# One decoder layer on one core: the key selection counted by sign sums on ScalarE alone, the mixers' queues laid out with other durations, and the next weights fetched through the mixers' feed

## The chip, the cores and the metric

The kernel runs on one core of a Trainium2 chip. Its engines work side by side, each through a queue of its own in a fixed order: TensorE (PE in the profile, its weight loads PEld), VectorE (DVE), ScalarE (ACT), GpSimd (POOL) and SyncE (SP, which only issues DMAs). The metric is the device time of one execution in microseconds (us): the median of three runs was 2349.24 us (2349.01 to 2350.36). Durations inside the kernel come from one profiled execution.

## The reference

One layer, 1024 tokens, width 1024, all in float32:

```
x = x + 1/2 * SwiGLU_1(RMSNorm(x))
h = RMSNorm(x);  [c_q|k_a|v_a|k_idx|w_idx|q_b|k_b|v_b|g_a|g_b] = h @ W_in
y_a: score[t,s] = sum over 8 heads of w_idx[t,h] * relu(q_idx[t,h] . k_idx[s])   (s <= t)
     the 256 keys of highest score of each token; softmax attention over those alone
y_b: a[t,s] = sigmoid(z[t,s]) * product over s < j < t of (1 - sigmoid(z[t,j])),  o = a @ v_b   (8 heads)
x = x + W_out( sigmoid(g_a) * (y_a @ W_oA) + sigmoid(g_b) * (y_b @ W_oB) )
x = x + 1/2 * SwiGLU_2(RMSNorm(x))
```

The selection is exact: of equal scores the keys that come first are taken until 256 are reached.

## The kernel before

A float32 product is made of three passes of matmuls on a high and a low part of each operand (`mm3`), and the two parts are written by a copy on ACT and a subtraction on DVE or POOL. The layer runs in five stretches: the first feed-forward block (0 to some 650 us), the projections and the **index stage** (to some 980 us), the **sticks stage** (stick-breaking attention, to some 1327 us), the **sparse stage** (attention over the selected keys, output products; to some 1565 us), and the second feed-forward block.

The three middle stages are written by hand: every piece of work is a generator (`Stream`) that names the engine and the tiles that it needs next, and a planner (`Weave`) steps the stream that could start first by its own clock. `Weave.cost` holds the durations that this clock uses; the order in which the streams are stepped is the order of the instructions in each engine's queue. A float in a `yield` is slack: such a piece stands back behind others that could start within that time.

Parts that the change touches:

- `topk` finds each token's 256th highest score. Tokens go in blocks of 128; blocks 0 and 1 have no more than 256 keys and need no search. **Group 0** is blocks 7, 2, 3 (1024, 384 and 512 keys), **group 1** blocks 4, 5, 6 (640, 768 and 896 keys). The threshold T is found bit by bit, 31 bits for each group. In `by_sign` a bit is one pass: for each block an ACT instruction takes the sign of score minus candidate over all keys and adds up the signs (tile `junka`, line 1108, with an accumulator read behind it), then DVE compares the three sums and sets the bit (`m`, `T`, `cand`, lines 1105 to 1112). Group 1 does 31 such passes, group 0 the upper 15. Its lower 16 bits are counted on DVE: the low halves of the scores whose upper half equals T are put in a tile `word`, and each bit is one DVE count for each block (tile `junkv`, line 1142).
- Where fewer than 256 scores are at or above zero, the search runs on negated scores: `flip` multiplies the score tiles (`u`) by `sig` (+1 or -1) before the search and again after it (line 1078).
- After the search, the **closing** of a group compares, counts, scans (`eq`, `gt`, `cum`, lines 1176 to 1189) and writes a tile of 0 and -1e30, `bias`, to DRAM (`bd`). The sparse stage's logits wait for both groups (`top0`, `top1`), and their DVE piece `e` (line 1699) reads the bias.
- `sticks`: for each head and half (c = 1 is token blocks 4 to 7, c = 0 blocks 0 to 3), scores on PE (`psz`), two sigmoids on ACT (`left`, `sa`), a product scan and a multiplication on DVE (`left`, `sa`), transposes on PE (`pstT`), their split on ACT and DVE (`pt`), products with the values (`psy`). `y_out` ends a half: it splits y into `yh` and `yl`, the subtraction being on POOL (line 1615).
- `fillers` are projections (`psf`) that PE does in between; `Feed` fetches and splits their weights, three sets ahead.
- At the end of the sparse stage `project("oa")` makes 8 outputs (`psoa`), each copied by ACT (`o`), multiplied and added on POOL and stored (`md`); behind them come the products `psm`, whose weights `woa` are fetched by `wcols` outside the planner.

Of the kernel before, what the change touches and what calls it, by code (L numbers as in the profile page):

```python
# [10 lines left out]
F32 = mybir.dt.float32  # L11
# [12 lines left out]
P = 128  # L24
# [6 lines left out]
H = 8  # L31
# [26 lines left out]
def f32(ap):  # L58
    return ap.bitcast(F32)
# [34 lines left out]
class Weave:  # L94
# [8 lines left out]
    COST = {PE: (0.015, 2400.0), DVE: (0.12, 960.0), ACT: (0.1, 1250.0), POOL: (0.2, 465.0)}  # L103

    def __init__(self, nc):
# [4 lines left out]
        self.streams, self.own, self.last = [], None, 0.0  # L110

    def cost(self, i, eng, outs, ins):
        fixed, rate = self.COST[eng]
        n = max([a.free_size() for a in outs[:1] + ins], default=1)
        if eng == PE:
            n = max(outs[0].free_size(), 240)
        else:
            fixed += (0.3 if eng == ACT else 0.08) * (len(outs) > 1)
        if eng == POOL and n <= H:
            fixed += 0.15 + 0.145 * n  # L120
        if eng == DVE:
            wide = [a for a in outs[:1] + ins if a.free_size() > 1]
            if getattr(i, "is_tensor_tensor_scan", False):
                n *= 2
            elif not any(a.space == PSUM for a in wide) and len(wide) <= 2:
                n *= (0.5 if any(a.dtype in (F32, F32R, I32) for a in wide) else 0.25) * len(outs)
        return fixed + n / rate
# [6 lines left out]
    def flush(self):  # L134
        traced = self.nc.cur_bb.bb.instructions
        for i in traced[self.seen:]:
# [6 lines left out]
            if any(a.space == DRAM for a in outs + ins):  # L143
                mb = prod(outs[0].shape) * 4e-6
                if eng == SP:
                    self.free[SP] = max(self.free[SP], t) + mb / 0.25
                    t, eng = self.free[SP] + 3.0, "DMA"
# [3 lines left out]
            else:  # L151
                t = max(t, self.free[eng]) + self.cost(i, eng, outs, ins)
# [68 lines left out]
def trunk(ctx, tc, x, positions, g_ffn1, w1_gate, w1_up, w1_down, g_mix, w_in, g_cq, w_uq_a, w_q_idx,  # L221
# [664 lines left out]
    with fp as fpool, fps as fpsum, psm as psum, tc.manual_schedule(  # L886
# [77 lines left out]
        sets += [(w, d * P, 2 * P, 0, 4, f"{nm}{d}") for w, nm in ((w_o_b, "ob"), (w_o_a, "oa")) for d in range(0, ND, 2)]  # L964

# [94 lines left out]
        def topk(group, gi):  # L1060
# [8 lines left out]
            def count(op, th):  # L1069
                for b, i in enumerate(group):  # L1070
                    yield DVE
                    nc.vector.tensor_scalar(junks[0][:, 0:(i + 1) * P], score[i], th if th == 0.0 else th[:, b:b + 1], 0.0,
                                            op0=op, op1=ALU.add, accum_out=cnt[:, b:b + 1])

            def flip():
                for b, i in enumerate(group):
                    yield DVE
                    nc.vector.tensor_scalar(score[i], score[i], sig[:, b:b + 1], None, op0=ALU.mult)

            def halves(b, i):  # L1080

                nk = (i + 1) * P
                return score[i].bitcast(U16)[:, 0:2 * nk:2], score[i].bitcast(BF16)[:, 1:2 * nk:2]

            yield DVE, *[f"score{i}" for i in group]
            yield from count(ALU.is_ge, 0.0)
# [3 lines left out]

            for b, i in enumerate(group):
                nk = (i + 1) * P
                a, d = (2 * TOPK - 1.0 - nk) / 2, (nk + 1.0) / 2
                c = slice(b, b + 1)
                nc.vector.tensor_scalar(kth[:, c], sig[:, c], a, d, op0=ALU.mult, op1=ALU.add)
                nc.vector.tensor_scalar(thr[:, c], kth[:, c], 2.0, -float(nk), op0=ALU.mult, op1=ALU.add)
            yield from flip()


            def by_sign(bits):  # L1100
# [15 lines left out]
            yield from by_sign(range(30, 15, -1))  # L1116
            if gi:
                yield from by_sign(range(15, -1, -1))
            else:
                yield DVE, "stick"  # L1120
                words = []

                above, low, clow = tl("above"), tl("low"), tl("clow")
                for b, i in enumerate(group):
# [941 lines left out]
```

## Time and profile before

| what | us |
|---|---|
| median of the runs (lowest, highest) | 2349.24 (2349.01, 2350.36) |
| the profiled execution's own time | 2345.06 |
| its span, first to last instruction | 2343.0 |
| busy in the span: PE, PEld, DVE, ACT, POOL | 2216.0, 1813.7, 1629.6, 1067.8, 935.9 |
| mean granted TensorE clock | 0.98 of full |

A busy share over the whole span mixes stages with different limits. The two feed-forward blocks are busy on PE nearly throughout and no line of them changes; the table by stage below is the one to read. Busy time of an engine counts overlapping instructions once. The cost of a DMA issue on ACT is not in its busy time.

### The profile page before, as it was taken

What the parts mean: (1) busy time and instruction counts of PE and PEld (TensorE: products, weight loads), DVE (VectorE), ACT (ScalarE), POOL (GpSimd) and SP (SyncE); (2) the same over time, 40 slices, a digit from 0 to 9 for tenths busy, and PEclk for the clock granted to TensorE, in tenths of its full rate; (3) what the DMA queues carried; (4) which work ended last, traced back from release to release, by engine and by line L of the source; (5) the groups of instructions that cost most, each with busy time, mean ns of one, the idle gap of its engine ahead of it and who ended that gap; (6) DMA issues with size and microseconds to landing.
All of it is one profiled execution on the core that took longest, in us unless ns stands there. A gap on an engine that the chain in (4) does not pass through costs nothing.

```text
span 2343.0 us, 30206 instructions
## 1 busy us (share of the span) xinstructions
PE 2216.0 (95%) x10460; PEld 1813.7 (77%) x10460; DVE 1629.6 (70%) x2596; ACT 1067.8 (46%) x2042; POOL 935.9 (40%) x675
## 2 busy tenths in 40 slices
PE   7999999999999988978998699979999999999999
PEld 6788888888888777756777588867878888888877
DVE  5765666688872688799989788833476666667675
ACT  4323233244462468766784565623332323233443
POOL 2554555332253433312332211376345555543233
PEclk9999999999999999998999899989999999999999
DMA  5233333586754323634454522457323333358755
GB/s 163 85 109 95 108 95 108 175 315 227 177 185 140 112 85 104 155 97 88 118 129 120 184 72 80 140 198 257 122 63 99 104 101 102 104 163 287 239 163 178
DMA packets 251497, 330.64 MB, mean 141 GB/s; under 512 B 19536, under 2 KB 154336, under 8 KB 251344
## 3 DMA queue, kind: packets, MB, share of 16 engines
q1 hardware_dynamic: 234224, 288.83, 40.6%
q0 software_dynamic: 7488, 24.16, 2.8%
q10 hardware_dynamic: 9632, 15.73, 1.9%
q8 instruction: 82, 1.34, 0.2%
q14 instruction: 71, 0.58, 0.1%
HBM read 234.78 MB, written 93.88 MB: 140 GB/s over the span
## 4 chain that ended last, share of the span: by engine, by line
PE 69%; DVE 16%; issue 5%; DMA 4%; ACT 4%; POOL 2%; SPq 0%; ACTq 0%; DVEq 0%; POOLq 0%
PE p L649 6%; PE p L650 6%; PE p L648 6%; PE pc L439 3%; PE pc L441 3%; PE pc L440 3%; PE pd L441 3%; PE pd L439 3%; PE pd L440 3%; PE pa L441 3%; PE pa L439 3%; PE pa L440 3%; DVE left L1549 2%; PE pb L439 2%; PE pb L441 2%
## 5 line engine op out<-in xcount | busy, mean ns | idle before, releaser
L1108 ACT ACTIVATE junka<-u,cand 128x640 bf16<-128x640 f32 (+1 forms) x138 | 124.5, 902 | 40.0 <-DVE cand L1105 35.3
L1549 DVE TENSOR_TENSOR_SCAN left<-left 128x640 f32<-128x640 f32 (+3 forms) x64 | 94.4, 1477 | 1.4 <-ACT left L1541 1.2
L1615 POOL TENSOR_TENSOR yl<-yl,yh 64x512 fp32r<-64x512 f32 x16 | 32.3, 2022 | 149.1 <-ACT yh L1611 149.1
L1649 PE MATMUL pstT<-ident,sa 128*128 128x128 f32 x288 | 52.0, 295 | 41.9 <-DVE sa L1552 28.9
L1649 PEld LDWEIGHTS pstT<-ident,sa 128*128 128x128 f32 x288 | 37.2, 150 | 57.1 <-DVE sa L1552 31.2
L1855 POOL TENSOR_TENSOR o<-o,gate 128x512 f32<-128x512 f32 x24 | 30.8, 1285 | 112.1 <-ACT o L1850 109.9
L1552 DVE TENSOR_TENSOR sa<-sa,left 128x639 f32<-128x639 f32 (+3 forms) x64 | 63.5, 994 | 3.4
L1596 ACT ACTIVATE pt<-pstT 128x512 fp32r<-128x512 f32 (+1 forms) x96 | 45.7, 491 | 43.9 <-PE pstT L1649 38.9
L1711 ACT ACTIVATE e<-e,nm 128x768 f32<-128x768 f32 (+7 forms) x64 | 49.4, 774 | 21.2 <-DVE nm L1706 20.6
L1598 DVE TENSOR_TENSOR pt<-pspT,pt 128x512 fp32r<-128x512 f32 x72 | 47.0, 685 | 16.3 <-ACT pt L1596 16.2
L1598 DVE TENSOR_TENSOR pt<-pstT,pt 128x512 fp32r<-128x512 f32 (+1 forms) x96 | 50.6, 548 | 10.5 <-ACT pt L1596 10.1
L1462 DVE SCALAR_TENSOR_TENSOR u<-relu,WI,u 128x512 f32<-128x512 f32 (+1 forms) x70 | 49.1, 716 | 10.2 <-ACT relu L1455 9.3
L649 PE MATMUL p<-bT,bS 128*128 128x512 f32 x132 | 52.7, 399 | 2.7 <-DVE bT L350 2.7
L650 PE MATMUL p<-bT,bS 128*128 128x512 f32 x132 | 52.4, 399 | 0.8 <-POOL bS L350 0.8
L1541 ACT ACTIVATE left<-psz 128x512 f32<-128x512 f32 (+2 forms) x96 | 46.1, 497 | 15.2 <-DVE sa L1552 6.2
L1699 DVE CUSTOM_DVE_ANT_0 e<-psL,bias 128x512 f32<-128x512 f32 (+3 forms) x96 | 50.0, 551 | 3.4 <-PE psL L1738 3.3
L649 PE MATMUL p<-aT,aS 128*128 128x512 f32 x132 | 51.7, 392 | 0.0
L650 PE MATMUL p<-aT,aS 128*128 128x512 f32 x132 | 50.9, 393 | 0.0
L1596 ACT ACTIVATE pt<-pspT 128x512 fp32r<-128x512 f32 x72 | 40.0, 594 | 22.4 <-PE pspT L1792 22.0
L1455 ACT ACTIVATE relu<-psdot 128x512 f32<-128x512 f32 (+1 forms) x80 | 39.6, 521 | 19.1 <-DVE u L1462 13.4
L1543 ACT ACTIVATE sa<-psz 128x512 f32<-128x512 f32 (+2 forms) x96 | 46.5, 502 | 3.5 <-ACT evg L1028 2.4
L648 PE MATMUL p<-bT,bS 128*128 128x512 f32 x132 | 46.4, 392 | 0.0
(3064 smaller groups left out, 8376.6 us busy)
## 6 DMA issues: line engine op xcount, KB each, us to landing
aw<-in_w_down_dram SPq DMA_DIRECT2D x33, 512.0 KB, 4.4
bw<-in_w_down_dram SPq DMA_DIRECT2D x33, 512.0 KB, 4.5
a0r<-in_w_gate_dram SPq DMA_DIRECT2D x22, 512.0 KB, 4.2
a1r<-in_w_up_dram SPq DMA_DIRECT2D x22, 512.0 KB, 4.7
b0r<-in_w_gate_dram SPq DMA_DIRECT2D x22, 512.0 KB, 4.0
b1r<-in_w_up_dram SPq DMA_DIRECT2D x22, 512.0 KB, 4.9
x<-in_x_dram SPq DMA_DIRECT2D x16, 512.0 KB, 6.1
gd<-evg ACTq DMA_DIRECT2D x32, 256.0 KB, 2.3
```

What stands on the lines that cost most here:

```text
L439: nc.tensor.matmul(ps, a[:, c], b[k][:, HI], start=start and k == 0, stop=False, skip_group_check=True)
L440: nc.tensor.matmul(ps, a[:, c], b[k][:, LO], start=False, stop=False, skip_group_check=True)
L441: nc.tensor.matmul(ps, a[:, l], b[k][:, HI], start=False, stop=k == 3, skip_group_check=True)
L648: nc.tensor.matmul(ps[q][m], S[:, h], T[:, HI], start=p == 0, stop=False)
L649: nc.tensor.matmul(ps[q][m], S[:, h], T[:, LO], start=False, stop=False)
L650: nc.tensor.matmul(ps[q][m], S[:, l], T[:, HI], start=False, stop=p == last)
L1108: nc.scalar.activation(junks[1][:, 0:(i + 1) * P], score[i], AF.Sign, bias=cand.bitcast(F32)[:, b:b + 1], accum_out=cnt[:, b:b + 1])
L1549: nc.vector.tensor_tensor_scan(back, back, back, 1.0, op0=ALU.mult, op1=ALU.bypass)
L1552: nc.vector.tensor_mul(a[:, 0:nk - 1], a[:, 0:nk - 1], left[:, 1:nk])
L1596: nc.scalar.activation(pt[:, off:512], tp[:, off:512], AF.Copy)
L1598: nc.vector.tensor_sub(pt[:, 512 + off:1024], tp[:, off:512], f32(pt[:, off:512]))
L1649: nc.tensor.transpose(tp[:, q * P:(q + 1) * P], A[n + q][:, j * P:(j + 1) * P], ident)
```

## The change

Three edits. (1) `topk`: group 0's lower 16 bits are counted by the same sign passes as the others, so that `word`, its counts and the accounts around them go; the scores are no longer turned, and instead each ACT sign instruction takes `scale=sig` beside its bias, and the closing works on the unturned scores with a corrected threshold (6 to 8 more instructions on 128x3 tiles for each group). A sign has slack 2.0. (2) `Weave.cost` gets other durations, a delay behind each result, a slower PE behind a pause, and a mutual slowing of DVE and POOL where both work in SBUF; so the order of all queues in the three middle stages changes, with the same work but for edit 1. In `y_out` the subtraction moves from POOL to DVE. (3) The first two `woa` weight sets are put behind the feed's list and fetched and split by it.

```diff
     def cost(self, i, eng, outs, ins):
-        fixed, rate = self.COST[eng]
+
         n = max([a.free_size() for a in outs[:1] + ins], default=1)
         if eng == PE:
-            n = max(outs[0].free_size(), 240)
...
+            return 0.01 + max(outs[0].free_size(), 240) / 2350, 0.0
+        if eng == ACT:
+            return 0.055 + n / 1190 + 0.22 * (len(outs) > 1), 0.1 + 0.15 * (len(outs) > 1)
...
+                cost, late = self.cost(i, eng, outs, ins)
+                if eng == PE:
+
+                    if t > self.free[PE] + 2.5:
+                        self.cold = 12
+                    self.cold -= 1
+                    cost += 0.85 * cost * (self.cold >= 0)
...
+                t += cost
                 self.free[eng] = self.last = t
+                t += late
...
+        sets += [(w_o_a, d * P, 2 * P, 0, 4, f"woa{d}") for d in (0, 2)]
...
-            yield from flip()
...
-                        yield ACT, cand, score[i]
+                        yield ACT, cand, score[i], 2.0
                         nc.scalar.activation(junks[1][:, 0:(i + 1) * P], score[i], AF.Sign,
-                                             bias=cand.bitcast(F32)[:, b:b + 1], accum_out=cnt[:, b:b + 1])
+                                             scale=sig[:, b:b + 1], bias=cand.bitcast(F32)[:, b:b + 1],
+                                             accum_out=cnt[:, b:b + 1])
...
-            yield from by_sign(range(30, 15, -1))
-            if gi:
-                yield from by_sign(range(15, -1, -1))
-            else:
...
-                for bit in range(15, -1, -1):
-                    nc.vector.tensor_scalar(clow, low, float(1 << bit), None, op0=ALU.add)
-                    for b, i in enumerate(group):
-                        yield DVE, 4.0
-                        nk = (i + 1) * P
-                        nc.vector.tensor_scalar(junks[0][:, 0:nk], words[b].bitcast(U16)[:, 0:nk], clow[:, b:b + 1], 0.0,
-                                                op0=ALU.is_ge, op1=ALU.add, accum_out=cnt[:, b:b + 1])
...
+            yield from by_sign(range(30, -1, -1))
...
-            yield POOL, yl, yh
-            nc.gpsimd.tensor_tensor(yl[0:HD], yt, f32(yh[0:HD]), op=ALU.subtract)
+            yield DVE, yl, yh
+            nc.vector.tensor_tensor(yl[0:HD], yt, f32(yh[0:HD]), op=ALU.subtract)
+            yield POOL, yl
             put_low(ybd[1][h * HD:(h + 1) * HD, cols], yt)
...
+        first = [feed().parts for n in range(2)]
...
-                wh, wl = wcols(w_o_a, d * P, 2 * P, 0, 4, f"woa{d}")
+                wh, wl = first.pop(0) if first else wcols(w_o_a, d * P, 2 * P, 0, 4, f"woa{d}")
```

Where the order moves, three places. The first is ACT's queue early in the sticks stage, between the first and the second head's sigmoids. Names with `cnt_6016` are group 0's signs, with `cnt_6023` group 1's. Before:

```order
L1541 ACTIVATE left<-psz 128x512 x2
L1543 ACTIVATE sa<-psz 128x512 x2
L1108 ACTIVATE junka,cnt_6023<-u_7221,cand_6028 128x640
L1541 ACTIVATE left<-psz 128x128
L1108 ACTIVATE junka,cnt_6023<-u_7538,cand_6028 128x768
L1543 ACTIVATE sa<-psz 128x128
L1108 ACTIVATE junka,cnt_6023<-u_7862,cand_6028 128x896
L1028 ACTIVATE evg<-psf 128x512
```

The same place in the changed program:

```order
L1526 ACTIVATE left<-psz 128x128
L1528 ACTIVATE sa<-psz 128x128
L1118 ACTIVATE junka,cnt_6023<-u_7854,cand_6028,sig_6024 128x896
L1118 ACTIVATE junka,cnt_6016<-u_6820,cand_6021,sig_6017 128x1024
L1118 ACTIVATE junka,cnt_6016<-u_7004,cand_6021,sig_6017 128x384
L1118 ACTIVATE junka,cnt_6016<-u_7131,cand_6021,sig_6017 128x512
L1581 ACTIVATE pt<-pstT 128x512 x2
```

Both groups' signs now stand between the sigmoids and the splits, up to six of them in a row. From the first `left` to the table load for the exponentials there are 75 signs in ACT's queue before, and 128 after.

The second place is DVE's queue where the sticks stage ends and the sparse stage's first `e` begins; `uvraw` is a tile laid over memory of the stage that ends. Before:

```order
L1598 TENSOR_TENSOR pt<-pstT,pt 128x512
L1607 TENSOR_TENSOR yl<-psy,yl 64x512
L1598 TENSOR_TENSOR pt<-pstT,pt 128x384
L1598 TENSOR_TENSOR pt<-pstT,pt 128x256
L1598 TENSOR_TENSOR pt<-pstT,pt 128x128
L1699 ISA e,mx<-psL,bias 128x512
```

The changed program:

```order
L1168 SCALAR_TENSOR_TENSOR eq<-cum,rem_11674,eq 128x768
L1170 TENSOR_TENSOR gt<-gt,eq 128x768
L1174 TENSOR_SCALAR cum<-gt 128x768
L1161 TENSOR_SCALAR eq<-u_7854,T_6027 128x896
L1163 TENSOR_SCALAR gt,cnt_6023<-u_7854,T_6027 128x896
L1164 TENSOR_SCALAR rem_11674<-cnt_6023 128x1
L1166 SCALAR_TENSOR_TENSOR cum<-eq 128x896
L1168 SCALAR_TENSOR_TENSOR eq<-cum,rem_11674,eq 128x896
L1170 TENSOR_TENSOR gt<-gt,eq 128x896
L1174 TENSOR_SCALAR cum<-gt 128x896
L1657 MEMSET uvraw 128x1024
L1685 ISA e,mx<-psL,bias 128x512
```

Group 1's closing, which before was spread among the last three heads, now stands whole behind the last splits and in front of the first `e`.

The third place is PE's queue at the end of the sparse stage, just ahead of the last products `psya` that the remaining `psoa` stand behind (`oa0` and `oa2` are weight sets). Before:

```order
L280 MATMUL psoa<-yah_11599,oa0h 128x512
L281 MATMUL psoa<-yal_11603,oa0h 128x512
L282 MATMUL psoa<-yah_11599,oa0l 128x512
L280 MATMUL psya<-oh_13815,uvh 128x256
L281 MATMUL psya<-ol_13816,uvh 128x256
```

The changed program:

```order
L302 MATMUL psoa<-yah_11448,oa2h 128x512
L303 MATMUL psoa<-yal_11452,oa2h 128x512
L304 MATMUL psoa<-yah_11448,oa2l 128x512
L302 MATMUL psya<-oh_13869,uvh 128x256
L303 MATMUL psya<-ol_13870,uvh 128x256
```

Before, 24 of the 96 `psoa` matmuls (two of the eight outputs) stand ahead of the last `psya`; after, 36 (three).

## Rows read from the trace of the kernel before

**Rows 1.** Windows by stage: us, busy of each engine (instructions), clock, DMA share, GB/s.

```profile
core 0: us, PE busy (x) PEld busy (x) DVE busy (x) ACT busy (x) POOL busy (x), PEclk, DMA share, GB/s
790.00:981.50 191.50, 169.03 (x823) 136.52 (x823) 156.47 (x304) 137.31 (x283) 74.32 (x69) 0.96 0.42 116
981.50:1326.80 345.30, 300.35 (x1467) 238.71 (x1466) 317.74 (x552) 237.13 (x509) 89.52 (x51) 0.94 0.47 122
1326.80:1352.00 25.20, 14.61 (x53) 10.08 (x52) 16.41 (x56) 12.58 (x22) 5.05 (x5) 0.66 0.36 102
1352.00:1515.00 163.00, 162.76 (x913) 139.08 (x913) 140.76 (x431) 105.35 (x229) 38.69 (x38) 1.00 0.27 87
1515.00:1565.00 50.00, 36.23 (x149) 28.19 (x148) 6.25 (x11) 12.49 (x20) 37.39 (x32) 0.86 0.71 244
```

**Rows 2.** Windows of single heads (1024-wide scan to the next), and ACT's fullest stretch.

```profile
998.90:1051.00 52.10, 42.35 (x199) 33.12 (x199) 50.26 (x109) 36.05 (x77) 9.56 (x6) 0.93 0.40 97
...
1271.80:1305.40 33.60, 29.65 (x158) 23.03 (x156) 30.93 (x40) 18.54 (x42) 6.23 (x4) 1.00 0.57 200
...
1185.00:1218.00 33.00, 30.89 (x164) 24.61 (x163) 27.87 (x50) 29.07 (x67) 6.88 (x6) 1.00 0.52 128
```

**Rows 3.** Groups by line on DVE, 780 to 1340 us: count, busy us, mean ns.

```profile
L1598 DVE TENSOR_TENSOR pt<-pstT,pt 128x512 fp32r<-128x512 f32 x48 | 31.8, 681 | 7.5 <-ACT pt L1596 7.3
...
L1142 DVE TENSOR_SCALAR_CACHE_REDUCE junkv<-word,clow 128x1024 bf16<-128x1024 uint16 x16 | 20.4, 1274 | 0.2
...
L1142 DVE TENSOR_SCALAR_CACHE_REDUCE junkv<-word,clow 128x512 bf16<-128x512 uint16 x16 | 11.8, 740 | 0.2
...
L1607 DVE TENSOR_TENSOR yl<-psy,yl 64x512 f32<-64x512 f32 x16 | 10.8, 677 | 2.2 <-ACT yl L1605 2.2
...
L1142 DVE TENSOR_SCALAR_CACHE_REDUCE junkv<-word,clow 128x384 bf16<-128x384 uint16 x16 | 9.7, 605 | 0.1
...
L1112 DVE SCALAR_TENSOR_TENSOR T<-m,T 128x3 int32<-128x3 int32 x46 | 8.6, 186 | 1.6
```

**Rows 4.** Groups by line on ACT: the signs (780 to 1340 us).

```profile
L1108 ACT ACTIVATION_READ_ACCUMULATOR junka<-u,cand 128x1 f32 x138 | 26.9, 195 | 0.0
...
L1108 ACT ACTIVATE junka<-u,cand 128x1024 bf16<-128x1024 f32 x15 | 17.3, 1153 | 10.5 <-DVE cand L1105 10.1 <-ACT evh L1016 0.4
L1108 ACT ACTIVATE junka<-u,cand 128x512 bf16<-128x512 f32 x15 | 10.8, 721 | 0.2
...
L1108 ACT ACTIVATE junka<-u,cand 128x384 bf16<-128x384 f32 x15 | 9.2, 615 | 0.4
```

**Rows 5.** Groups on ACT, whole span: a PSUM copy with a scale column, and without.

```profile
L330 ACT ACTIVATE mhi<-pst,gcolm 128x512 fp32r<-128x512 f32 x16 | 9.8, 694 | 0.0
...
L349 ACT ACTIVATE aT<-pst 128x512 fp32r<-128x512 f32 x16 | 8.3, 598 | 16.1 <-PE pst L399 16.1
```

**Rows 6.** Windows, 1205 to 1290 us: DVE on tile `eq`: us, busy, clock, DMA, GB/s.

```profile
1205.00:1290.00 85.00, 14.88 (x12) 0.98 0.47 127
```

**Rows 7.** Groups on DVE, 1205 to 1291 us.

```profile
L1072 DVE TENSOR_SCALAR_CACHE_REDUCE junkv<-u,cand 128x640 bf16<-128x640 f32 (+2 forms) x3 | 3.0, 1006 | 0.0
...
L1178 DVE TENSOR_SCALAR_CACHE_REDUCE gt<-u,T 128x640 f16<-128x640 f32 (+2 forms) x3 | 3.0, 997 | 0.0
```

**Rows 8.** Timeline of the turn to the sparse stage; in brackets the wait ahead.

```profile
1337.40 0.91 DVE L1671 MEMSET uvraw<- 128x1024 f32 x1 [3.23 <-issue]
...
1339.59 0.63 PE L1792 MATMUL pspT<-ident,e 128*128 128x128 f32 x2
```

**Rows 9.** Instructions on `bd`, DMA from issue to landing.

```profile
DMA to landing us min/median/max: 1.9/2.9/8.2
```

**Rows 10.** The page: groups, whole span.

```profile
L1699 DVE CUSTOM_DVE_ANT_0 e<-psL,bias 128x512 f32<-128x512 f32 (+3 forms) x96 | 50.0, 551 | 3.4 <-PE psL L1738 3.3
```

**Rows 11.** Waits from 1515 to 1565 us: in total, times, longest.

```profile
ACT o L1850 <- DMA md<-o: 12.7, 3, 7.3
...
PE psm L280 <- ACT o L1850: 9.2, 1, 9.2
```

More of the change, by code (lines that the diff above doesn't have):

```diff
@@ L110, in __init__ @@
         self.streams, self.own, self.last = [], None, 0.0
+        self.cold, self.shared, self.sbuf = 0, [], 0.0
     def cost(self, i, eng, outs, ins):
-        fixed, rate = self.COST[eng]
         n = max([a.free_size() for a in outs[:1] + ins], default=1)
         if eng == PE:
-            n = max(outs[0].free_size(), 240)
-        else:
[L118 to L127, printed above, removed]
+            return 0.01 + max(outs[0].free_size(), 240) / 2350, 0.0
+        if eng == ACT:
+            return 0.055 + n / 1190 + 0.22 * (len(outs) > 1), 0.1 + 0.15 * (len(outs) > 1)
+        if eng == POOL:
+            return 0.2 + n / 465 + (0.15 + 0.145 * n) * (n <= H), 0.0
+        wide = [a for a in outs[:1] + ins if a.free_size() > H]
+        if not wide:
+            return 0.12 + 0.1 * (len(ins) > 1), 0.08
+        if getattr(i, "is_tensor_tensor_scan", False):
+            return 0.1 + n / 480, 0.08
+        if len(outs) > 1:
+            return 0.13 + n / 960, 0.05
+        if len(wide) == 2 and not any(a.space == PSUM for a in wide):
+            return 0.17 + n * (0.5 if any(a.dtype in (F32, F32R, I32) for a in wide) else 0.25) / 960, 0.08
+        return 0.07 + n / 960, 0.08
     def hop(self, name, eng):
@@ L151, in flush @@
             else:
-                t = max(t, self.free[eng]) + self.cost(i, eng, outs, ins)
+                cost, late = self.cost(i, eng, outs, ins)
[4 more added lines that the diff above has]
+                    cost += 0.85 * cost * (self.cold >= 0)
+                t = max(t, self.free[eng])
+                if not any(a.space == PSUM for a in outs + ins) and max(a.free_size() for a in outs + ins) > H:
+                    pace = 0.5 if len(reads) < 2 else 0.1
+                    if eng == POOL:
+                        self.shared = self.shared[-3:] + [(t, t + cost)]
+                        self.free[DVE] += (1 - pace) * min(cost, max(self.sbuf - t, 0.0))
+                    if eng == DVE:
+                        for a, z in self.shared:
+                            cost += max(min((z - max(a, t)), (t + cost - max(a, t)) / pace), 0.0) * (1 - pace)
+                        self.sbuf = t + cost
+                t += cost
                 self.free[eng] = self.last = t
+                t += late
             for n in writes:
@@ L1067, in topk, with count @@
             T, cand, m = tl("T", I32), tl("cand", I32), tl("m", I32)
-            def count(op, th):
+            def count(th):
                 for b, i in enumerate(group):
@@ L1158, in topk @@
             Tf, cf = T.bitcast(F32), cand.bitcast(F32)
-            yield from count(ALU.is_ge, cf)
-            fix = tl("fix")
+            fix, up, edge = tl("fix"), tl("up"), tl("edge")
+            nc.vector.tensor_scalar(up, sig, 0.0, None, op0=ALU.is_gt)
+            nc.vector.tensor_tensor(edge, cf, Tf, op=ALU.subtract)
+            nc.vector.tensor_tensor(fix, edge, up, op=ALU.mult)
+            nc.vector.tensor_tensor(fix, Tf, fix, op=ALU.add)
+            nc.vector.tensor_tensor(fix, fix, sig, op=ALU.mult)
+            yield from count(fix)
+            nc.vector.tensor_tensor(cnt, cnt, sig, op=ALU.mult)
             nc.vector.tensor_tensor(fix, cnt, kth, op=ALU.is_ge)
```

45 lines of the change are left out of this document (6 added, 39 removed).

## The prediction

> **What bounds the kernel now.** I read the windows by stage first, since a busy share over the whole span mixes stages with different limits; then the windows of single heads, the groups by line, the chain of waits and the timeline where one stage turns into the next. The sparse stage is PE's: 162.76 of 163.00 us [rows 1]. The sticks stage, 345.30 us, is not: DVE is busy for 317.74 us of it (0.92), PE for 300.35 at clock 0.94, ACT for 237.13 [rows 1]. It isn't even, either. The first head takes 52.10 us with DVE busy for 50.26; a late one takes 33.60, with PE at 29.65 of them [rows 2]. The reader is to see in the instruction counts why: the first heads carry the DVE counts of group 0 as well. So DVE bounds the first half of the stage, and in the second half DVE and PE are close. In the tail of the sparse stage nobody is full: PE works for 36.23 of 50.00 us [rows 1], ACT's copies `o` wait 12.7 us in all for the stores of `md`, and the first `psm` waits 9.2 us for `o` [rows 11].
>
> **Edit 1 on DVE.** Sixteen bits less, each of three counts: 16 x (1.274 + 0.605 + 0.740) = 41.9 us [rows 3]. The sixteen subtractions `yl` come to DVE; I price them by the PSUM subtraction of the same shape, 16 x 0.677 = 10.8 us [rows 3], an upper bound, as SBUF operands cost no more here. DVE in the sticks stage falls from 317.7 to 317.7 - 41.9 + 10.8 = 286.6 us; the flips, the words and the counts' accumulator reads that go too I leave uncounted, as they only loosen an engine that no longer binds.
>
> **Edit 1 on ACT.** The order has 75 signs between the first `left` and the exponentials' table load before, and 128 after. Forty-eight of the 53 are group 0's sixteen bits: 16 x (1.153 + 0.615 + 0.721 + 3 x 0.195) = 49.2 us [rows 4]. The other five move in from the index stage: about 5 x 0.9 = 4.5. The second pointer operand (`scale=sig` beside the bias) the trace does not show on a sign. The nearest rows are two copies of 128x512 out of PSUM, 0.694 us with a scale column and 0.598 without [rows 5], so it costs between nothing and 0.096 each; a gain I exclude, since the instruction does nothing less. I take the row's value: 128 x 0.096 = 12.3 us. ACT then has 237.1 + 49.2 + 4.5 + 12.3 = 303.1 us of work in the stage. Of this, 3 come off, since the busy rows count overlapping instructions once and a sum of means doesn't (my choice; the rows don't say how much), and some 9 stand behind the last sign in the new order (sixteen splits, copies and sigmoids of 128 to 512 columns, the widest at 0.598 [rows 5]). So 291 lie ahead of it. ACT is now the fullest engine, ahead of PE's 300.35 over the whole stage, and a fixed order of three engines with nearly equal loads can't be packed full. By the share that the bounding engine reached over the whole stage before (0.92) [rows 1] the last sign ends 291 / 0.92 = 316 us after the stage's start. The share of ACT's own fullest stretch, 29.07 of 33.00 us [rows 2], is 0.88 and gives 331; that of DVE's best head, 50.26 of 52.10 [rows 2], is 0.96 and gives 303. I take 316.
>
> The Trainium skill ("ScalarE: Activation LUTs", section "What ACT_TABLE_LOAD costs") says that each [128,1] pointer operand adds about 93 ns to an ACTIVATE; by that the term would be 128 x 0.093 = 11.9 us instead of 12.3. It agrees with the one pointer of rows 5, and no run here shows a second one on a sign, where it speaks against this change.
>
> **The closing of group 1.** Before, it lay spread between 1205 and 1290 us, beside the last heads. In the new order it stands whole behind the last splits, and the first `e` and `uvraw` stand behind it on DVE: there is no cover for it any more. Its DVE work from the last sign on: tile `eq` 14.88 us [rows 6], two sets of counts of 3.0 each [rows 7], the three writes of the bias some 1 us; 28 small instructions at 0.186 [rows 3], 5.2; and the pieces that still stand among them, four `yl` at 0.677 and ten `pt` of which none costs more than the 0.681 of the widest [rows 3], at most 9.5, of which I take 7. That is 14.9 + 6.0 + 1.0 + 5.2 + 7 = 34 us. Then the last bias goes out and comes back by DMA (2.9 us median for `bd` [rows 9]) and `uvraw` is written (0.91 [rows 8]): 4. Then eight `e` at 0.551 [rows 10], an exponential and its division ahead of the first `pspT`: 6. So the first `pspT` comes 316 + 34 + 4 + 6 = 360 us after the stage's start; before, it came at 1339.59 [rows 8], 358.1 us after 981.50. The sticks stage with its turn costs **+2 to +3**: what DVE lost in counts is taken up by ACT and by the bare closing. With 303 it is -11, with 331 +17.
>
> PE has little to do in those 44 us, and there the clock shows: in the turn before, PE was busy for 14.61 of 25.20 us at a granted clock of 0.66 [rows 1], with matmuls at the 1.2 GHz level among them. I expect the same, for longer.
>
> **Edits 2 and 3.** In the index stage PE is busy for 169.03 of 191.50 us [rows 1]. Five signs, group 1's and 0's flips and the words' preparation leave it, and ACT's first signs wait 10.5 us ahead of them, mostly for DVE's `cand` [rows 4]. Neither engine binds the stage, so I take **-4**, between -10 (that wait gone) and +2. Behind the first `pspT` both groups' biases are ready and the twelve or so us to the sparse stage's full pace can shrink a little: **-2** (-5 to 0). In the tail the order puts three instead of two of the eight `psoa` outputs ahead of the last `psya`, so that one store fewer stands between the last `o` and `psm`; a third of the 12.7 us of waits for `md` [rows 11] is **-4** (-6 to 0). The two `woa` sets fetched by the feed are issued earlier, but the order leaves ACT's `o` and their splits in the same places, and `psm` waited for `o`, not for weights [rows 11]: 0 (-2 to +2). What hides them is the same sparse stage; if it didn't, `psm` would already be waiting for weights in the trace. The rest, both feed-forward blocks and the 162.76 us of the sparse stage [rows 1], is unchanged.
>
> **Sum.** -4 + 3 - 2 - 4 = -7 us against the profiled execution's own 2345.06: 2338. The median of the runs, 2349.24, lies 4.2 above that execution, so the forecast carried to it is **2342 us**. About 0.2%, or 4.7 us, is what a measurement here can tell from no change: faster means below 2344.5, slower above 2353.9.
>
> **Rivals.** (A) *The new order packs better.* With ACT at 0.96 the last sign ends at 303, the stage costs -11; with -10 in the index stage, -4 and -6 behind, the sum is -31: 2318 us. For it: each engine has under 304 us of work in a stage that took 345, and the first heads' DVE bound, 52.10 against 33.60 us a head [rows 2], goes. Against it: no window of ACT shows more than 0.88, and PE's and ACT's loads are now equal. (B) *ACT becomes the bound and the closing is bare (slower).* ACT fills to no more than 0.88, the last sign ends at 331, nothing covers the 44 us behind it, the index stage gains nothing and the tail 2: +17 - 2 = +15, 2364 us. With those terms it is measurably slower once the last sign ends later than about 321 us from the stage's start. For it: up to six signs stand in a row in front of splits for which PE's products wait, ACT's best share so far is 0.88 [rows 2], and the closing's place is read from the order. Against it: DVE, 31 us looser, can answer ACT's splits at once. (C) *The second pointer costs nothing.* ACT has 12 us less, 279 / 0.92 = 303 for the last sign, the sum -11 - 4 - 2 - 4 = -21: 2328 us. For it: a sign reads its bias by a pointer already, and the second may be read beside it. Against it: the row of one scale pointer [rows 5]. (D) *The change doesn't do what it says*: the sign passes stay hidden by nothing and the better order is no better, so that -41.9 on DVE only meets another limit; the time is within 0.2% of 2349.
>
> **How the numbers follow.** My forecast 0.35 (its own range 2334 to 2350, from -15 to +1 by the terms' smaller bounds), A 0.22, B 0.25, C 0.10, D 0.08. Faster: A and C whole, and half of the forecast's 0.35, 0.18: 0.50. Same: half of what is left of the forecast, all of D and a little of B's near side: 0.22. Slower: the rest, 0.28: B, and the forecast's upper edge. The range reaches from A's 2318 to a little over B's 2364, and leaves the outer half of A and the outer part of B, some 0.2, beyond: 2318 to 2366.
>
> **What would show it.** Right: no count `junkv` but the closings' and the first ones is left on DVE; DVE's share of the sticks stage falls from 0.92 to near 0.8 and ACT's rises from 0.69 to above 0.85; the sign of 1024 takes about 1.25 us instead of 1.153; the first heads take 40 to 43 us; the last sign ends near 316 us after the first `left`, and behind it lies a block of some 34 us of DVE with PE mostly idle at the lower clock, and the first `pspT` near 360. Wrong: a sign of 1.15 us (C); a last sign before 306 us or the closing overlapped by heads (A); a last sign after 321, and waits of PE for `pt` behind signs (B); a tail as long as before (then 4 us of the sum are missing), or `psm` waiting for weights.

## The result, and the profile after

The changed kernel takes 2322.36 us (median of four runs, 2321.67 to 2323.18) against 2349.49 for the kernel before (median of four, 2349.01 to 2350.36): a ratio of 0.9884, with a 95% interval of 0.9867 to 0.9901. The forecast was 2342, in a range of 2318 to 2366. The time lies in the range and on the side that was forecast, but the forecast step of -7 us is a quarter of the measured -27. Most of the rest comes from something that the forecast did not contain: 32 bytes.

The profiled execution has a span of 2320.1 us (before 2343.0). Cut at instructions that both kernels have, the two spans, and four of the experiments below, come apart like this (us; each column sums to its span):

| stretch | before | before again (e0) | before, tiles 32 B higher (e4) | changed | changed, tiles 32 B lower (e5) | new order, old selection, 32 B higher (e6) |
|---|---|---|---|---|---|---|
| start to the first matmul on `aA` (first feed-forward block) | 469.8 | 469.4 | 462.9 | 463.6 | 469.4 | 463.1 |
| to the first scan of `left` | 511.7 | 513.7 | 509.5 | 498.7 | 501.1 | 499.6 |
| to the first `pspT` | 358.1 | 358.9 | 359.6 | 371.3 | 371.8 | 358.5 |
| to the last `psya` | 183.6 | 183.3 | 183.2 | 183.7 | 185.7 | 183.7 |
| to the first `psm` | 32.2 | 32.2 | 33.1 | 23.0 | 23.6 | 23.2 |
| to the end | 787.6 | 787.3 | 781.7 | 779.8 | 788.7 | 778.2 |

From before to changed, the six rows give -6.2, -13.0, +13.2, +0.1, -9.2 and -7.8. The first and the last, 14 of the 23 us, are nearly all feed-forward blocks, in which the change alters nothing.

The sticks stage went much as worked out. Windows of the changed kernel: from the first scan to the start of the last sign, from there to the write of `uvraw`, and on to the first `pspT` (columns as in [rows 1]):

```profile
962.30:1282.00 319.70, 289.84 (x1429) 228.71 (x1430) 239.42 (x417) 285.17 (x608) 50.71 (x33) 0.96 0.50 125
1282.00:1317.30 35.30, 11.98 (x47) 8.66 (x45) 29.91 (x67) 7.87 (x17) 2.77 (x5) 0.58 0.35 117
1317.30:1333.60 16.30, 8.35 (x26) 6.04 (x27) 10.46 (x40) 7.37 (x12) 2.34 (x1) 0.65 0.22 65
```

ACT is busy for 285.17 of 319.70 us (0.89); DVE, at 0.92 of the stage in [rows 1], is at 0.75. Behind the last sign lies a block of 35.3 us in which DVE works for 29.91 and PE for 11.98, at a granted clock of 0.58 of full. Two windows of single heads, the first and a late one, show the change of bound. In the first, DVE's 50.26 us of 52.10 in [rows 2] have become 28.34 of 41.43, with PE and ACT now next to each other at the top. In the late one ACT and DVE are the fullest, and the head takes 37.70 us, where the late head of [rows 2] took 33.60.

```profile
976.19:1017.62 41.43, 39.95 (x199) 30.95 (x198) 28.34 (x51) 38.01 (x82) 6.66 (x4) 1.00 0.46 112
...
1234.11:1271.81 37.70, 29.82 (x155) 22.83 (x153) 33.12 (x57) 34.30 (x73) 7.54 (x7) 0.94 0.59 205
```

The groups by line on ACT, from 780 to 1340 us of the changed kernel, answer to [rows 4]: the sign of 1024 keys costs 1252 ns, 99 more than with one pointer.

```profile
L1118 ACT ACTIVATE junka<-u,cand,sig 128x1024 bf16<-128x1024 f32 x31 | 38.8, 1252 | 5.8 <-DVE cand L1115 4.3 <-DVE pt L1583 0.4 <-ACT evh L1039 0.4
L1118 ACT ACTIVATION_READ_ACCUMULATOR junka<-u,cand,sig 128x1 f32 x186 | 37.3, 201 | 0.0
```

The end of the stage was not worked out well. The timeline of the changed kernel there (start, duration, engine; in brackets the wait ahead) answers to [rows 8]:

```profile
1317.34 0.91 DVE L1657 MEMSET uvraw<- 128x1024 f32 x1 [2.95 <-DMA bd<-cum]
1318.17 0.63 DVE L1685 CUSTOM_DVE_ANT_0 e<-psL,bias 128x512 f32<-128x512 f32 x1
...
1323.71 1.06 ACT L1662 ACTIVATE uvh<-uvraw 128x1024 fp32r<-128x1024 f32 x1 [22.36 <-DMA uvraw<-in_w_uv_a_dram]
1324.78 1.28 ACT L1695 ACT_TABLE_LOAD   x1
1326.08 0.94 ACT L1697 ACTIVATE e<-e,nm 128x768 f32<-128x768 f32 x1
...
1333.64 1.05 PE L1778 MATMUL pspT<-ident,e 128*128 128x128 f32 x7
```

DVE's first `e` begins at 1318.17, but the first exponential on ACT only at 1326.08. In front of it on ACT stand the table load and `uvh`, and `uvh` waits for the weights that a DMA brings into `uvraw` behind DVE's memset. From the end of the first division, at 1327.96, another 5.7 us pass: thirteen `e` and three divisions, not eight and one, are done ahead of the first `pspT`. So 15.5 us pass from the first `e` to the first `pspT`, not the 6 that the forecast gave.

In the tail the waits of the changed kernel, from 1510 to 1550 us, are nearly those of [rows 11], though the stretch is 9 us shorter:

```profile
ACT o L1836 <- DMA md<-o: 10.6, 2, 7.4
...
PE psm L302 <- ACT o L1836: 8.9, 1, 8.9
```

What went lies ahead of that wait. In the window from the last `psya` to the first `psm`, POOL has 16 instructions and 19.62 us in the changed kernel, and had 22 and 25.27: more of the outputs are out of the way when the stretch begins. First the changed kernel, then the one before:

```profile
1517.30:1540.30 23.00, 14.11 (x63) 11.25 (x61) 0.57 (x2) 6.32 (x9) 19.62 (x16) 0.85 0.63 208
```

```profile
1523.20:1555.40 32.20, 18.86 (x76) 14.12 (x74) 0.85 (x2) 6.95 (x10) 25.27 (x22) 0.86 0.72 244
```

### The profile page after: what moved, and what is told of

Read it like the earlier page. It is cut to its first block, busy times and chain, and to the rows that moved or that the text cites. A ratio compares the mean times of both kernels' runs of the same rounds, so it can differ in the third digit from the quotient of the medians.

```text
span 2320.1 us, 30206 instructions
## 1 busy us (share of the span) xinstructions
PE 2190.6 (94%) x10460; PEld 1814.1 (78%) x10460; DVE 1577.2 (68%) x2497; ACT 1114.3 (48%) x2138; POOL 901.1 (39%) x659
## 4 chain that ended last, share of the span: by engine, by line
PE 69%; DVE 10%; issue 7%; ACT 7%; DMA 4%; POOL 2%; ACTq 0%; SPq 0%; DVEq 0%; POOLq 0%
PE p L671 5%; PE p L672 5%; PE p L670 5%; PE pc L461 3%; PE pc L463 3%; PE pc L462 3%; PE pd L463 3%; PE pd L461 3%; PE pd L462 3%; PE pa L463 3%; PE pa L461 3%; PE pa L462 3%; ACT junka L1118 3%; PE pb L463 2%; PE pb L461 2%
## 5 line engine op out<-in xcount | busy, mean ns | idle before, releaser
L1118 ACT ACTIVATE junka<-u,cand,sig 128x1024 bf16<-128x1024 f32 (+5 forms) x186 | 182.5, 981 | 14.8 <-DVE cand L1115 4.7
L1602 POOL DMA_DIRECT2D ybld<-yl x16 | 8.8, 547 | 147.6 <-DVE yl L1600 122.0
L1723 PE MATMUL psL<-kkh,qs 128*128 128x512 f32 (+2 forms) x96 | 38.2, 404 | 25.1 <-DVE mx L1685 25.0
L671 PE MATMUL p<-bT,bS 128*128 128x512 f32 x132 | 51.8, 393 | 2.9 <-DVE bT L372 2.8
L1537 DVE TENSOR_TENSOR sa<-sa,left 128x639 f32<-128x639 f32 (+3 forms) x64 | 51.7, 811 | 3.0
L672 PE MATMUL p<-bT,bS 128*128 128x512 f32 x132 | 51.5, 393 | 1.0 <-POOL bS L372 1.0
L1440 ACT ACTIVATE relu<-psdot 128x512 f32<-128x512 f32 (+1 forms) x80 | 40.9, 522 | 20.3 <-DVE u L1447 13.2
```

Of the source, the lines that this page charges most:

```text
L671: nc.tensor.matmul(ps[q][m], S[:, h], T[:, LO], start=False, stop=False)
L672: nc.tensor.matmul(ps[q][m], S[:, l], T[:, HI], start=False, stop=p == last)
```

## The experiments

Each ratio is against runs of the kernel before on the same chip.

**e0, the kernel before once more**, without an edit.

> The kernel before, unchanged, for a trace beside the others of this chip. In the first two traces the second feed-forward block, whose instructions are the same in both kernels, took 668.5 us before and 658.7 after (from the last write of x to the end), with a matmul of 512 columns at 395 against 389 ns. Theory P (that is a property of the execution or the chip, not of the program): here the same program shows a block nearer to 659, at least 3 us below 668.5. Theory Q (the program's code or its place decides): 668 again. Time 2345 to 2350 by Q, 2337 to 2342 by P.

Measured: 2346.93 us; 666.8 us from the last write of x to the end, with three in five of the matmuls in it at 392 to 397 ns. Theory Q, as far as one more execution shows it: the program decides.

**e1, the new order with the old selection** (`topk` of before; the rest as changed).

```diff
-            yield from by_sign(range(30, -1, -1))
+            yield from by_sign(range(30, 15, -1))
+            if gi:
+                yield from by_sign(range(15, -1, -1))
+            else:
...
```

> Edits 2 and 3 as changed, but the selection of the kernel before (turned scores, group 0's lower 16 bits counted on DVE, no slack on a sign). Theory T1 (the order from the new durations gives the gain; the selection is about even, since ACT gets what DVE loses): 2320 to 2332 us, faster than before by 0.7% or more, first left at most 970 us. Theory T2 (the selection gives the gain, by taking 42 us of counts off DVE): 2340 to 2352, and the first heads take 50 us again.

Measured: 0.9931 (0.9917 to 0.9945), 2331.95 us, at the edge of T1's range, with the first `left` at 970.7 us. The feed-forward blocks have the pace of before (469.6 us to `aA`), but from `aA` to `psm` it needs 1073.0 us, against 1085.6 before and 1076.7 in the changed kernel.

**e2, the new selection with the old order.**

```diff
-            return 0.01 + max(outs[0].free_size(), 240) / 2350, 0.0
...
+    COST = {PE: (0.015, 2400.0), DVE: (0.12, 960.0), ACT: (0.1, 1250.0), POOL: (0.2, 465.0)}
...
```

> Edits 1 and 3 and the subtraction yl on DVE as changed, but the planner's old durations and old step. T1: 2340 to 2355 us, the index stage as long as before (first scan near 981). T2: 2320 to 2332, the first scan near 962.

Measured: 0.9941 (0.9927 to 0.9954), 2333.77 us, between the two expectations, and now with the higher pace of the feed-forward blocks (463.1 us to `aA`). Neither expected the first scan at 947.6 us: the stretch from `aA` to the first scan is the shortest of all runs (484.5 us), the one from there to the first `pspT` the longest (393.8), and both together take 8 us more than in the changed kernel. This gave the next theory: the blocks have the higher pace in every program with the new selection and the lower one in every program with the old. The new selection leaves one constant tile more in the pool that is laid out first, and by the program's allocation every later tile of the low side of SBUF then lies 32 bytes higher.

**e3, edit 3 undone.**

```diff
-        sets += [(w_o_a, d * P, 2 * P, 0, 4, f"woa{d}") for d in (0, 2)]
...
-        first = [feed().parts for n in range(2)]
...
-                wh, wl = first.pop(0) if first else wcols(w_o_a, d * P, 2 * P, 0, 4, f"woa{d}")
+                wh, wl = wcols(w_o_a, d * P, 2 * P, 0, 4, f"woa{d}")
```

> The changed kernel without edit 3: the first two woa sets fetched and split outside the planner as before. My step (edit 3 is worth nothing, as psm waits for ACT's o and its stores): 2320 to 2325 us, the time from the last psya to the first psm within 2 us of 23.2. Rival (the tail's 9 us are edit 3's): 2329 to 2333, that time back near 32.

Measured: 0.9898 (0.9884 to 0.9911), 2324.23 us, and 22.8 us from the last `psya` to the first `psm`. The tail's 9 us are not edit 3's. They come with the order: the stretch takes 23.6 us in e1 and 34.0 in e2, with edit 3 in both.

**e4 and e5, the 32 bytes alone.** e4 is the kernel before with an unused constant tile; e5 is the changed kernel with two of its constant tiles laid into one. The queues and their order stay the same, but for one memset in e4.

```diff
 # e4, on the kernel before
+    nc.vector.memset(cst.tile([P, 8], F32, name="pad0"), 0.0)
 # e5, on the changed kernel, for group 0 alone
-            fix, up, edge = tl("fix"), tl("up"), tl("edge")
+            fix = tl("fix")
+            both = cst.tile([P, 2 * n], F32, name=f"upedge{gi}")
+            up, edge = both[:, 0:n], both[:, n:2 * n]
```

> The kernel before with one more constant tile of 32 bytes a partition ahead of all the others that follow, so that every later tile of the low side of SBUF lies 32 bytes higher (32 instead of 0 modulo 64); the five queues are the same, but for one memset of that tile at the start. Theory S (the two feed-forward blocks ran 6 and 9 us faster in the changed kernel because edit 1 leaves one constant tile more, which moves all tiles by 32 bytes): the block behind the mixers takes 659 instead of 667 to 668.5 us, its matmuls 389 instead of 395 ns, time 2331 to 2338. Theory R (something else of the program does it, as the code of the selection): 2345 to 2351, matmuls at 395.

> The changed kernel with two of its new constant tiles of group 0 (up, edge) laid into one, so that every later tile lies 32 bytes lower, where the kernel before had it; the queues are the same. Theory S: matmuls of the feed-forward blocks at 395 ns, the last block 667 to 669 us, time 2334 to 2339. Theory R: 2320 to 2325.

Measured: e4 0.9931 (0.9919 to 0.9943), 2331.19 us; e5 0.9988 (0.9980 to 0.9996), 2344.79 us. Theory S on both, with e5 some us above its range. Windows from 100 to 400 us, inside the first feed-forward block, for before, changed, e4 and e5 (columns as in [rows 1]; read the count behind PE's busy time):

```profile
100.00:400.00 300.00, 300.00 (x1303) 244.15 (x1302) 186.58 (x204) 92.59 (x159) 159.31 (x111) 1.00 0.32 100
```

```profile
100.00:400.00 300.00, 300.00 (x1325) 248.44 (x1324) 194.15 (x207) 93.05 (x162) 162.87 (x113) 1.00 0.33 104
```

```profile
100.00:400.00 300.00, 300.00 (x1325) 248.40 (x1324) 192.66 (x206) 92.39 (x160) 163.20 (x113) 1.00 0.34 105
```

```profile
100.00:400.00 300.00, 300.00 (x1303) 244.12 (x1302) 187.08 (x204) 92.27 (x158) 160.21 (x111) 1.00 0.32 100
```

A busy share and a granted clock of 1.00 hide it: the same 300 us hold 1303 matmuls in one placement and 1325 in the other, 1.7% more. Single groups of matmuls tell more. In the first feed-forward block one operand of each matmul, the one of 128 columns that PEld loads, lies, by the program's allocation, on the low side of SBUF or on the high side, which the edit does not move; the other operand always lies on the high side. Two groups next to each other, 140.8 to 147 us of the kernel before: the loaded operand of `pb` is on the low side, that of `pd` on the high side.

```profile
L440 PE MATMUL pb<-aT,a12S 128*128 128x512 f32 x4 | 1.6, 395 | 0.0
...
L440 PE MATMUL pd<-aT,a12S 128*128 128x512 f32 x4 | 1.6, 389 | 0.0
```

The same two in e4, 139 to 147 us:

```profile
L441 PE MATMUL pd<-aT,a12S 128*128 128x512 f32 x4 | 1.6, 389 | 0.0
...
L441 PE MATMUL pb<-aT,a12S 128*128 128x512 f32 x4 | 1.6, 389 | 0.0
```

In the kernel before it is the matmuls with a loaded operand on the low side that are slow, and in e4, where that side lies 32 bytes higher, they are as fast as the others.

**e6, the new order, the old selection and the higher place** (e1 with e4's tile).

> The new order with the selection of before (run e1_old_selection) and the constant tile of 32 bytes as well. Theory S: 15 us below that run, 2314 to 2320, so below the changed kernel's 2322, which would say that edit 1 costs time and that the rest gives it. Theory R: 2329 to 2335.

Measured: 0.9847 (0.9833 to 0.9860), 2311.81 us, the fastest kernel of all, 2 us below Theory S's range and 10.6 us below the changed one. So edit 1 costs time in the new order: e6 to changed, and e1 to e5, are the same step at either placement, +11 and +13 us. In the old order it costs next to nothing: e4 to e2, both at the higher place, is +2.6 us, with overlapping intervals (e2 also has edit 3 and `yl` on DVE). The two edits have no prices of their own.

**e7 and e8, signs with one pointer.** All 31 bits by signs, but on scores that DVE turns before the search and back after it. In e7 the tiles lie 128 bytes below the changed kernel's, in e8 at the same addresses.

```diff
+            yield from flip()
...
-                                             scale=sig[:, b:b + 1], bias=cand.bitcast(F32)[:, b:b + 1],
+                                             bias=cand.bitcast(F32)[:, b:b + 1],
```

> The changed kernel with all 31 bits still counted by ScalarE, but on turned scores: sig is multiplied into the score tiles on DVE before and after the search, as before, and the sign has its bias as the only pointer. Tiles lie at 32 modulo 64, as in the changed kernel. My step (the second pointer costs 0.1 us on each of 128 signs of the sticks stage, ACT is full there): the last sign ends 8 to 14 us sooner after the first scan, 2310 to 2318 us. Rival (ACT's signs do not set the stage's end, or the twelve multiplications on DVE take it back): 2319 to 2326.

> Run e7_turned_scores with four unused constant tiles, so that all later tiles lie at exactly the changed kernel's addresses. In e7 they lay 128 bytes lower and the feed-forward blocks showed the slow pace again (434 matmuls of 512 columns in a full 100 us, against 443). Theory S2 (the address decides, and 32 modulo 64 is not the rule): 443 again, and 13 to 18 us less than e7: 2317 to 2322; the selection on turned scores then is 0 to 5 us faster than the changed kernel. Rival (turning itself costs the 12 us): 2331 to 2337.

Measured: e7 0.9945 (0.9932 to 0.9958), 2334.52 us, with 1300 matmuls in the window of 300 us; e8 0.9858 (0.9842 to 0.9875), 2315.47 us, with 1325. Neither expectation for e7 held; Theory S2 did, with e8 some 1.5 us below its range. The 128 bytes are worth 19 us, and 32 modulo 64, which e7 and e8 share, is not the rule. At equal addresses turning is 7 us faster by the medians (the intervals overlap a little), and the trace agrees: 364.3 us from the first scan to the first `pspT`, against 371.3. The last sign comes hardly sooner after the first scan (318.1 against 319.7 us): my step expected 8 to 14 us there, and more signs stand behind the first `left` in e8 (134 by the order, against 128). The gain lies behind the last sign: from there to the first `pspT` e8 takes 46.2 us, the changed kernel 51.6. The sign of 1024 keys with one pointer, in e8:

```profile
L1135 ACT ACTIVATE junka<-u,cand 128x1024 bf16<-128x1024 f32 x31 | 35.8, 1155 | 2.5 <-DVE cand L1132 1.7 <-ACT yh L1606 0.5
```

**e9, a fourth place**: e5's edit for both groups, so 64 bytes below the changed kernel.

```diff
-            fix, up, edge = tl("fix"), tl("up"), tl("edge")
+            fix = tl("fix")
+            both = cst.tile([P, 2 * n], F32, name=f"upedge{gi}")
+            up, edge = both[:, 0:n], both[:, n:2 * n]
```

> The changed kernel with up and edge laid into one tile for both groups: later tiles 64 bytes lower than in the changed kernel, the queues the same. If every odd multiple of 32 bytes were fast: 2320 to 2325 and 443 matmuls in a full 100 us. If only the changed kernel's place (32 bytes below a multiple of 4096, where the tiles of the high side lie too) is fast: 2335 to 2346 and 434 or 435.

Measured: 0.9946 (0.9932 to 0.9961), 2336.25 us. The window holds 1317 matmuls, between the two paces, so neither expectation holds: the pace has more than two levels, and no rule of 64 bytes fits.

```profile
100.00:400.00 300.00, 300.00 (x1317) 246.85 (x1316) 189.85 (x206) 92.54 (x160) 162.30 (x112) 1.00 0.33 103
```

**e10, half of group 0's lower bits on DVE.**

```diff
+                yield from by_sign(range(30, 7, -1))
...
+                for bit in range(7, -1, -1):
+                    nc.vector.tensor_scalar(cand, T, 1 << bit, None, op0=ALU.bitwise_or)
+                    for b, i in enumerate(group):
+                        yield DVE, 4.0
+                        nc.vector.tensor_scalar(junks[0][:, 0:(i + 1) * P], score[i], cf[:, b:b + 1], 0.0,
+                                                op0=ALU.is_ge, op1=ALU.add, accum_out=cnt[:, b:b + 1])
```

> New order, addresses of the changed kernel, turned scores; group 0's lower 8 bits are counted on DVE (on the scores themselves, no words), its other 23 and all of group 1 on ACT. In the queues 100 signs stand behind the first left, and both groups' closings stand beside heads, the last bias before the last head ends. Theory L (the changed kernel loses 10 us to the same order with the old selection because ACT is full and group 1's closing stands bare behind it): the time from the first scan to the first pspT falls below 350 us, 2296 to 2308 us in all. Rival (DVE and ACT share the work in any split with the same result): 2310 to 2322.

Measured: 0.9889 (0.9874 to 0.9904), 2322.43 us. Theory L fails. The last sign begins 113 us ahead of the first `pspT` and the closings stand beside heads, but the first `pspT` still comes 362.8 us after the first scan, and the stretch from there to the last `psya` takes 188.1 instead of 183.7. Against e8, which has the same addresses and turned scores, the first of these stretches is 1.5 us shorter and the whole 7 us longer by the medians; e10 also leaves out the slack on a sign, so the split of the counting is not the only difference. Windows from the first scan to the first `pspT`, of e10, then of e6 and e8:

```profile
964.00:1326.80 362.80, 308.98 (x1469) 243.41 (x1470) 302.72 (x560) 267.18 (x574) 55.40 (x39) 0.90 0.47 121
```

```profile
962.70:1321.20 358.50, 304.74 (x1487) 242.94 (x1486) 313.10 (x618) 254.24 (x542) 56.97 (x39) 0.91 0.48 124
```

```profile
963.30:1327.60 364.30, 301.22 (x1475) 236.85 (x1475) 281.83 (x523) 290.77 (x641) 54.05 (x39) 0.90 0.47 122
```

From e6 to e8 DVE goes from 313 to 282 us and ACT from 254 to 291, and the stretch moves by 6. No engine is above 0.88, and PE is at 0.83 to 0.85 in all three: a fairer split of the counting buys nothing more.

**e11, the subtractions `yl` back on POOL** (on e6).

```diff
-            yield DVE, yl, yh
-            nc.vector.tensor_tensor(yl[0:HD], yt, f32(yh[0:HD]), op=ALU.subtract)
-            yield POOL, yl
+            yield POOL, yl, yh
+            nc.gpsimd.tensor_tensor(yl[0:HD], yt, f32(yh[0:HD]), op=ALU.subtract)
```

> Run e6_old_selection_plus32 (the fastest so far: new order, selection of before, edit 3, the changed kernel's addresses) with the sixteen subtractions yl back on POOL, so the last part of edit 2 undone. DVE is busy for 313 of the 358.5 us from the first scan to the first pspT in e6, and the subtractions take 16 x 0.68 = 10.9 us of that. If DVE still sets the pace there: 6 to 11 us less, 2301 to 2306. Rival (no engine is the bound any more at a share of 0.87, and the subtraction takes 1.3 us or more on POOL and is later for it): 2309 to 2316.

Measured: 0.9865 (0.9845 to 0.9885), 2315.35 us: no gain, 3.5 us more by the medians, with overlapping intervals. DVE gives away sixteen instructions and is busy for longer, 320.98 us against e6's 313.10:

```profile
962.00:1324.00 362.00, 307.10 (x1486) 244.36 (x1487) 320.98 (x607) 255.45 (x544) 88.28 (x55) 0.90 0.48 124
```

The time went into DVE's other instructions. The narrowest scans, first in e6, then in e11:

```profile
L1573 DVE TENSOR_TENSOR_SCAN left<-left 128x128 f32<-128x128 f32 x8 | 3.3, 414 | 0.0
```

```profile
L1573 DVE TENSOR_TENSOR_SCAN left<-left 128x128 f32<-128x128 f32 x8 | 7.2, 902 | 0.0
```

Of the eight in e11, five take 409 to 422 ns; the three beside which POOL does a subtraction take 724, 1779 and 2633.

## Why the prediction was right, and where it was wrong

The three edits as argued, without the 32 bytes, are e5 against the kernel before: a ratio of 0.9988, so -2.8 us of 2348, with an interval of -4.7 to -0.9. With the tiles at the higher place in both (e4 against changed), the medians differ by 8.8. The forecast's -7 lies between the two, partly by luck: its terms failed in opposite directions. What remains, 16 us (e4) to 22 us (e5), is the placement, which the sum did not contain.

- **ACT's term** held. The second pointer costs 97 ns at 1024 keys (1252 against e8's 1155), where 96 was taken from the row of a scale column, so rival C falls. The Trainium skill ("ScalarE: Activation LUTs", section "What ACT_TABLE_LOAD costs") gives about 93 ns for each pointer operand; this case's trace agrees within 4. The last sign begins 319.7 us after the first scan, where 316 was forecast for its end. Two small errors offset each other there: ACT is busy for 285 us ahead of it, not 291, and fills the stage to 0.89, not the 0.92 that was taken.
- **DVE's term was too high.** Forecast were 286.6 us in the stage; 269.3 were measured up to `uvraw`. The sixteen `yl` alone cost more than their "upper bound" of 10.8 us: 14.1. Thirteen of them take 656 to 684 ns, as priced, and the three that run beside a subtraction on POOL 1374 to 2486. Since DVE no longer bound the stage, neither error reached the sum.
- **The closing** held: 35.3 us from the start of the last sign to `uvraw`, the wait for `bd` included, with PE at a third and its granted clock at 0.58. Forecast were 34 and 2.9.
- **The last term of that sum failed.** "Then eight `e` at 0.551, an exponential and its division ahead of the first `pspT`: 6" measured 15.5. The exponential stands behind `uvh` and the table load in ACT's queue, and `uvh` behind a DMA; and more `e` stand ahead of the first `pspT` than were counted. The trace of before gave the length, though not this cause: the first `e` was at 1326.79 us and the first `pspT` at 1339.59 [rows 8], 12.8 us later. There the first exponential followed at once, and DVE then stood for 3.23 us in front of `uvraw` [rows 8]. So the first `pspT` came at 371.3, for 360 forecast. The first `e` and the first exponential of the kernel before:

```profile
1326.79 0.68 DVE L1699 CUSTOM_DVE_ANT_0 e<-psL,bias 128x512 f32<-128x512 f32 x1
...
1328.59 0.94 ACT L1711 ACTIVATE e<-e,nm 128x768 f32<-128x768 f32 x1 [0.74 <-DVE nm L1706]
```

- **The index term was too small.** From `aA` to the first scan e5 is 10.6 us below the kernel before at the same placement, where -4 (-10 to +2) was given; by luck that pays for most of the miss above. The reason given, work of edit 1 that leaves the stage, was not needed for it: with the old selection, whose turning and words stay, the new order alone gives 9.9 us in the same stretch (e4 to e6), and the new selection 0.9 more (e6 to changed). The tail was too small as well: -8.6 in e5, where -4 (-6 to 0) was given. The waits for `md`, a third of which were to go, fell only from 12.7 to 10.6 us; the rest is work that the order puts ahead of the tail. Edit 3 at nothing held (e3), and -2 at the sparse start did not come.
- **"The rest, both feed-forward blocks ..., is unchanged" failed.** The instructions are, but PE's pace in them is not. This is why the time landed near rival A's 2318 while A's mechanism did not occur: ACT did not pack to 0.96, and the stage grew longer.
- **The order** (edit 2, here with edit 3, which is worth nothing) brings the gain proper. With the old selection, e1 against the kernel before is -16.6 us at the lower place, e6 against e4 -19.4 at the higher; with the new selection, changed against e2 is -11.4. **Edit 1** costs 11 to 13 in the new order. The traces place that ahead of the first `e`, which comes 343.1 us after the first scan in e6 and 355.8 in the changed kernel: what rival B described, at a smaller price. About 7 us of it go with scores turned as before (e8), mostly behind the last sign, so the second pointer on the signs is not shown to be the cause. For the rest my theory was the bare closing, which e10 does not bear out. The rest stays open and is within the intervals.

One after the other at the higher place: placement -16.5 (before to e4), order with `yl` and edit 3 -19.4 (e4 to e6), selection +10.6 (e6 to changed). These are consecutive steps between medians, so they add up to the whole by construction and do not test it; in another sequence, by way of e2, the last two would be priced at +2.6 (selection with `yl` and edit 3, e4 to e2) and -11.4 (order, e2 to changed).

## What to carry to other kernels

When stretches whose code did not change get faster, count the matmuls in a window that PE fills: a busy share of 1.00 at full clock does not say how fast it goes. A constant tile more or less can outweigh a change of schedule, so two schedules are compared at equal tile addresses, if need be with an unused tile. A price found for one edit holds for the order that it was measured in: the selection cost 11 us in one order and some 3 in the other. And the way into a new stage is followed through each engine's queue, not through the data alone: the first exponential here had its operands some 6 us before its turn.

## What the runs showed of the hardware that was not expected

- PE's pace in matmuls of 512 columns depends on where the tiles lie in SBUF; 32 bytes are enough to change it. By the allocation the low side's tiles of 4096 bytes in the feed-forward blocks begin 3936 (e7), 4000 (e9), 4032 (before, e5) or 4064 bytes (changed, e4, e6, e8) above a multiple of 4096; 300 us that PE fills hold 1300, 1317, 1303 and 1325 matmuls. The high side's tiles, `mhi` for one, lie at 4064 in all of them, so the best of these four places is the one where both sides agree. The traces also say which access it is. From 100 to 400 us of the kernel before, one matmul starts 233.3 ns behind the other on average where both load their 128-column operand from the low side (667 times), and 226.8 where both load it from the high side (537 times); in e4 both take 226.7. Work of DVE, ACT or POOL at the same time makes no difference: 230.3 to 230.6 ns with and without, for each of them. So it is the place of the operand that PEld loads. Whether that place counts by itself or against the other operand, which never moved, stays open, and so does why 64 bytes below (e9, 229.0 ns) cost less than 32 (233.3) or 128 (e7, 232.7).
- A subtraction on POOL lengthened DVE's own work: sixteen of 64x512 took 10.8 us in DVE's list and, moved to POOL, left DVE busy for 7.9 us more (e11 against e6). One such meeting in the changed kernel, where a `yl` alone takes some 680 ns:

```profile
1090.95 2.39 POOL L962 TENSOR_TENSOR wg0l<-wg0r,wg0h 128x1024 fp32r<-128x1024 f32 x1 [21.73 <-ACT wg0h L960]
1091.41 2.49 DVE L1600 TENSOR_TENSOR yl<-yl,yh 64x512 fp32r<-64x512 f32 x1 [1.03 <-ACT yh L1596]
```
